# The state space stage of a hybrid encoder layer, reordered as a pipeline over pairs of heads, with the PSUM banks shared out anew

## The chip, the cores and the metric

One core of one Trainium2 chip runs the whole layer as one program. The metric is the device time of one execution in microseconds; lower is better. The kernel before takes 2852.92 us (median of three runs, 2851.68 to 2853.5). One execution was also taken by the hardware profiler; it took 2852.71 us, and 2850.9 us of that lie between its first and its last instruction (the span).

## The reference

One layer of a streaming encoder works on 384 tokens: 256 frames of a new stream and 8 running streams with 16 frames each. All is float32. The part that matters here is branch B, a state space model over 64 heads in 8 groups:

```python
proj = u @ p['w_in']                    # pool | z | x,B,C | dt | gates
xbc  = silu(causal_conv(xbc) + b)
dt   = softplus(dt_raw + dt_bias);  A = -exp(a_log)
def step(h, inp):                       # one chunk of 64 frames, all heads
    cum   = jnp.cumsum(dtc * A, axis=1)
    decay = jnp.exp(jnp.where(causal, cum[:, :, None] - cum[:, None, :], -jnp.inf))
    cb    = jnp.einsum('btgn,bsgn->btsg', Cc, Bc)
    xdt   = xc * dtc[..., None]
    y = einsum('btsgr,bsgrp->btgrp', cb[..., None] * decay, xdt)
    y = y + einsum('btgn,bgrpn->btgrp', Cc, h) * jnp.exp(cum)[..., None]
    h = h * exp(last) + einsum('bsgn,bsgr,bsgrp->bgrpn', Bc, exp(last - cum), xdt)
...
y = y + d_skip * xh
a_ssd = rmsnorm_per_group(y * silu(z)) * ssd_norm
m = sigmoid(g_A) * (A @ w_pool_proj) + sigmoid(g_B) * (a_ssd @ w_ssd_proj)
x += rmsnorm(m @ w_out);  x += rmsnorm(relu(rmsnorm(x) @ w_up)**2 @ w_down)
```

The outputs are the 384 tokens and the new pooling, convolution and state space states.

## The kernel before

**Matrix products.** Channels lie on the partitions and the 384 tokens along the free axis. A weight comes as units of 128x1024 float32 by the DMA queue of the sync engine (SP), through three buffers (`wfetch`, L62). ScalarE rounds it to the type fp32r (`wh`, L72), VectorE computes what is lost by that (`wl`, L74); both go through three buffers too. One 128x128 block then takes three matmuls, `wh*xh`, `wh*xl` and `wl*xh` (`mm3`, L80 to L83). A projection of 128 channels (`proj`, L94) reads two units and is 48 matmuls of 128x384 into one PSUM bank.

**Order.** A scheduler at build time orders each engine's instructions by its own estimate of when their inputs are ready; the engines then issue in that fixed order and wait on semaphores. `tc.issue_after` (`behind`, L59) keeps one instruction behind another on its engine. A pool gives out its buffers in the order in which the program asks.

**PSUM.** The eight banks are two pools of four: `psm` (`mmtile`) for all projections and for the products of the MLP, `pss` (`sstile`) for transposes, norms and the state space products.

**Stages in order.** First the tokens are loaded and the first projections run, with the input norm `rstd`. Then come the pooling branch (`pool_tile`, `pool_map`: tiles pj_p, pw, dh), gates (pj_ga), `dt_phase` (L291) and the pooling output (pj_pp). `dt_phase` computes softplus and the cumulated sums on VectorE (L299 to L329) and transposes the results with eleven small transposes to PSUM (`tk`, L341), from which `tok` is copied.

Then the state space stage, L409 to L601, loops over eight groups of heads:

- ten projections: B and C (`conv`: evacuation, convolution of four taps, SiLU), four x (also `conv`), four z;
- B's transposes (`trB`, L428), from which `Bk` and, by way of DRAM, the block-diagonal `bst` are made; C masked by stream (`Cm`); the products B C (`cb`, L452), masked to `cbm`;
- for each of two pairs of 128 channels (four heads): the old state `hs` and the cumulated sums `cbc` are loaded; x is transposed (`trx`, L475) and scaled to `xdt` and `xdw`; `yi` (L480) is C times the old state, eight products of 32 columns; the decays `E` (128x2048, L500 to L515) are made on ScalarE and VectorE; `Y` (L528) is twelve products of `xdt` with `E`; `yis`, the scaled yi, is added to Y by a product with the identity (L538); `pp` (L542) is the new state of the first stream; `su` (L581) that of the other eight, from `bst` and from `xst`, which also goes by way of DRAM (`xscr`);
- `finish` (L586): the norm over the group (`norm_bc`, with its product `bc`), the results to DRAM;
- one gate projection (`gate_b`) in the first six groups, the others behind the loop.

trB, trx, cb, yi, Y, L538 and pp are true float32 products; projections and su are fp32r. The program writes a group's products behind its ten projections; the scheduler then mixes them with the projections that follow.

Last come the output of branch B (pj_sp), w_out (wo), the second norm and the MLP. At the MLP's entry, x1 is transposed tile by tile (`trm`, L727), split to `x1h` and `x1l`, and its squares are summed on ScalarE (L743) for the norm, whose product `bc` is at L749; the first MLP projection (pj_up, L763) follows in the program.

Of the kernel before, what the change touches and what calls it, by code (L numbers as in the profile page):

```python
# [14 lines left out]
P = 128  # L15
T = 384
# [18 lines left out]
def build(ctx, tc, io):  # L35
# [5 lines left out]
    psm = ctx.enter_context(tc.tile_pool(name="psm", bufs=4, space=PSUM))  # L41
    pss = ctx.enter_context(tc.tile_pool(name="pss", bufs=4, space=PSUM))
# [41 lines left out]

    def half(o, q, wl_, rhs):
        h, l = wl_
        for k in range(8):
            i = q * 8 + k
            c = slice(k * P, k * P + P)
            last[0] = mm3(o, h[:, c], l[:, c], rhs[i][0], rhs[i][1], i == 0, i == len(rhs) - 1)  # L90

    last = [None]
# [69 lines left out]
    wt = mmtile("warm_o")  # L162
# [16 lines left out]
    ps = mmtile("pj_p0")[:, :T]  # L179
    ps1 = mmtile("pj_p1")[:, :T]  # L180
# [27 lines left out]
    with tc.tile_pool(name="phc", bufs=1, reuse_waits="tile") as pc, tc.tile_pool(name="phc2", bufs=2, reuse_waits="tile") as pc2:  # L208
# [153 lines left out]
    with tc.tile_pool(name="phd", bufs=2, reuse_waits="tile") as pd, tc.tile_pool(  # L362
# [46 lines left out]
        for g in range(G):  # L409
            u0 = 49 + g * 10  # L410
            BT = conv(u0, 32 + g, "BT", 2)
            CT = conv(u0 + 1, 40 + g, "CT", 2)
            xs = []
            for j in range(4):
                xs.append(conv(u0 + 2 + j, g * 4 + j, "xs", 6))
                if g and j == 2:
                    finish(last[0])
            zs = []
            for j in range(4):
# [4 lines left out]
                zs.append(z)  # L424

            tr = sstile(f"trB{g}")
            for b in range(3):
                te.transpose(tr[:, b * P : b * P + P], BT[:, b * P : b * P + P], ident)  # L428
            Bk = pd.tile([P, 2, P], F32, tag="Bk", name=f"Bk{g}")
            s.copy(Bk.rearrange("p b n -> p (b n)"), tr[:, :TP])  # L430
            Bhl = pd.tile([P, 2, P], F32R, tag="Bhl", name=f"Bhl{g}", bufs=1)
            s.activation(Bhl[:, 0, :], tr[:, TP:T], AF.Copy)
            v.tensor_tensor(Bhl[:, 1, :], tr[:, TP:T], Bhl[:, 0, :].bitcast(F32), ALU.subtract)
            bscr = b_scr[g]
            sy.dma_start(bscr, Bhl.bitcast(F32))
            bs = bst[g % 2]
            for p4 in range(4):
                for h2 in range(2):
                    sy.dma_start(
                        bs[p4 * 32 + h2 * 16 : p4 * 32 + h2 * 16 + 16, :, h2, :].bitcast(F32),  # L440
                        bscr.rearrange("(q h r) l n -> h l r q n", q=4, h=2)[h2, p4 // 2],
                    )
            Cm = pd.tile([P, 2, P], F32, tag="Cm", name=f"Cm{g}")
            v.tensor_tensor(
                Cm,
                CT[:, TP:].unsqueeze(1).to_broadcast([P, 2, P]),
                cst[:, C_CM : C_CM + 256].rearrange("p (a t) -> p a t", a=2),
                ALU.mult,
            )
            cb = sstile(f"cb{g}")  # L450
            for sb, t0, c0, n in ((0, 0, 0, 256), (1, P, 256, P), (2, TP, T, P)):
                te.matmul(  # L452
                    cb[:, c0 : c0 + n], BT[:, sb * P : sb * P + P], CT[:, t0 : t0 + n], start=True, stop=True
                )
            cbm = pd.tile([P, 512], F32, tag="cbm", name=f"cbm{g}")
            v.tensor_tensor(cbm, cb, cst[:, C_MASK : C_MASK + 512], ALU.mult)

            ssum = pd.tile([P, T], F32, tag="ssum", name=f"ssum{g}", bufs=1)
            for jp in range(2):
                nm = f"{g}_{jp}"  # L460
                qd = g * 2 + jp
                h0 = qd * 4
                js = (jp * 2, jp * 2 + 1)
                hs = pd.tile([P, NB, 2 * P], F32, tag="hs", name=f"hs{nm}")
                sy.dma_start(hs, io["ssm"][qd])
                cbcs = []
                for q in range(2):
                    cbc = pd.tile([P, 2, T], F32, tag="cbc", name=f"cbc{nm}_{q}")
                    sy.dma_start(cbc, cum_scr[h0 + q * 2 : h0 + q * 2 + 2, :].partition_broadcast(P))
                    cbcs.append(cbc)  # L470
                trs = []
                for j in js:
                    tr = sstile(f"trx{g}_{j}")
                    for b in range(3):
                        te.transpose(tr[:, b * P : b * P + P], xs[j][:, b * P : b * P + P], ident)  # L475
                    trs.append(tr[:, :T].rearrange("p (b h q) -> p b h q", b=3, h=2))
                yi = sstile(f"yi{nm}")
                for c in range(4):
                    for r in range(2):
                        te.matmul(  # L480
                            yi[c * 32 : c * 32 + 32, :256],
                            Cm[:, r, c * 32 : c * 32 + 32],
                            hs[:, 2 * c + r, :],
                            start=r == 0,
                            stop=r == 1,
                        )
                xdt = pd.tile([P, 2, 3, P], F32, tag="xdt", name=f"xdt{nm}", bufs=1)
                xdw = pd.tile([P, 2, 3, P], F32, tag="xdw", name=f"xdw{nm}", bufs=1)
                for q, tv in enumerate(trs):
                    for o, i in ((xdt, 3), (xdw, 6)):  # L490
                        v.tensor_tensor(
                            o[:, q].rearrange("p b (h q) -> p b h q", h=2),
                            tv,
                            tok[:, i : i + 3, h0 + q * 2 : h0 + q * 2 + 2].unsqueeze(3).to_broadcast([P, 3, 2, 64]),
                            ALU.mult,
                        )
                xhl = pd.tile([P, 2, 2, P], F32R, tag="xhl", name=f"xhl{nm}", bufs=1)
                s.activation(xhl[:, 0], xdw[:, :, 2, :], AF.Copy)
                v.tensor_tensor(xhl[:, 1], xdw[:, :, 2, :], xhl[:, 0].bitcast(F32), ALU.subtract)
                E = pd.tile([P, 4, 512], F32, tag="E", name=f"E{nm}", bufs=1)  # L500
                for hh in range(4):
                    ch = cbcs[hh // 2][:, hh % 2]
                    s.activation(E[:, hh, P:TP], ch[:, P:TP], AF.Exp, bias=tok[:, 9, h0 + hh : h0 + hh + 1])
                    for b, e0 in enumerate((0, TP, T)):
                        v.tensor_scalar(
                            E[:, hh, e0 : e0 + P],
                            ch[:, b * P : b * P + P],
                            tok[:, b, h0 + hh : h0 + hh + 1],
                            0.0,
                            ALU.subtract,  # L510
                            ALU.min,
                        )
                s.activation(E[:, :, :P], E[:, :, :P], AF.Exp)
                s.activation(E[:, :, TP:], E[:, :, TP:], AF.Exp)
                v.tensor_tensor(E, E, cbm.unsqueeze(1).to_broadcast([P, 4, 512]), ALU.mult)  # L515
                yis = pd.tile([P, 2, P], F32, tag="yis", name=f"yis{nm}", bufs=1)
                v.tensor_tensor(
                    yis.rearrange("p j (h q) -> p (j h) q", h=2),
                    yi[:, :256].rearrange("p (h q) -> p h q", h=4),
                    tok[:, 10, h0 : h0 + 4].unsqueeze(2).to_broadcast([P, 4, 64]),  # L520
                    ALU.mult,
                )
                Ys = []
                for q in range(2):
                    Y = sstile(f"Y{nm}_{q}")
                    for sb, e0, c0, n in ((0, 0, 0, TP), (1, TP, P, P), (2, T, TP, P)):
                        for hh in range(2):
                            te.matmul(  # L528
                                Y[hh * 64 : hh * 64 + 64, c0 : c0 + n],
# [65 lines left out]
            if g == G - 1:  # L595
                finish(None)
            if g < NG:
                gate_b()
# [331 lines left out]
```

## Time and profile before

| what | value |
|---|---|
| median of three runs | 2852.92 us |
| profiled execution | 2852.71 us |
| its span | 2850.9 us |
| matmul records | 15855 |
| granted TensorE clock, mean | 0.998 |
| VectorE, ScalarE, GpSimd busy | 55%, 38%, 4% |
| chain that ended last: share of TensorE | 96% |
| one group of heads, from 648.34 to 754.70 | 106.36 us |
| from there, VectorE and ScalarE busy | 81.82 us, 48.93 us |

In the profile, PE is the TensorE matmul and PEld its weight load, DVE is VectorE, ACT ScalarE, POOL GpSimd and SP the sync engine. A timeline line has the start in us, the length, the engine, the line of the kernel, the operation, what it writes and reads, shapes and count; in square brackets stand the idle time ahead of it and what ended that. Matmuls are pipelined, so that a record is longer than the distance to the next start; the starts tell the pace. A float32 product has two records, a transpose or an fp32r product one. A line of the table by stretches has the stretch, its length, the busy time of PE, PEld, DVE, ACT and POOL with their counts, the granted TensorE clock (1.00 is full), the share of the DMA engines and GB/s.

### The profile page before, as it was taken

What the parts mean: (1) busy time and instruction counts of PE and PEld (TensorE: products, weight loads), DVE (VectorE), ACT (ScalarE), POOL (GpSimd) and SP (SyncE); (2) the same over time, 40 slices, a digit from 0 to 9 for tenths busy, and PEclk for the clock granted to TensorE, in tenths of its full rate; (3) what the DMA queues carried; (4) which work ended last, traced back from release to release, by engine and by line L of the source; (5) the groups of instructions that cost most, each with busy time, mean ns of one, the idle gap of its engine ahead of it and who ended that gap; (6) DMA issues with size and microseconds to landing.
All of it is one profiled execution on the core that took longest, in us unless ns stands there. A gap on an engine that the chain in (4) does not pass through costs nothing.

```text
span 2850.9 us, 39369 instructions
## 1 busy us (share of the span) xinstructions
PE 2828.8 (99%) x15855; PEld 2676.3 (94%) x15855; DVE 1569.1 (55%) x2235; ACT 1081.7 (38%) x1554; POOL 105.0 (4%) x156
## 2 busy tenths in 40 slices
PE   8999999999999999999999999999999999999998
PEld 7999999999999999999999987989898998989897
DVE  7674335678778778777533334534444444444445
ACT  5343224345345345344422233533232333323233
POOL 0000000001001001011000000000000000000000
PEclk9999999999999999999999999999999999999999
DMA  6444445466466466466644453343343343344333
GB/s 204 138 133 142 137 138 195 143 213 213 155 211 217 156 206 219 159 212 231 205 152 155 143 182 115 133 131 126 128 129 128 126 130 129 126 128 130 127 126 126
DMA packets 141655, 448.78 MB, mean 157 GB/s; under 512 B 17200, under 2 KB 40816, under 8 KB 136864
## 3 DMA queue, kind: packets, MB, share of 16 engines
q1 hardware_dynamic: 133152, 410.14, 44.4%
q0 software_dynamic: 8320, 36.13, 3.3%
q8 instruction: 124, 2.03, 0.3%
q14 instruction: 59, 0.48, 0.1%
HBM read 404.48 MB, written 41.72 MB: 157 GB/s over the span
## 4 chain that ended last, share of the span: by engine, by line
PE 96%; DVE 2%; issue 1%; ACT 1%; DMA 0%; SPq 0%; DVEq 0%; ACTq 0%
PE pj_up L82 6%; PE pj_up L83 6%; PE pj_up L81 6%; PE wd L645 6%; PE wd L644 6%; PE wd L646 6%; PE pj_x L81 5%; PE pj_x L83 5%; PE pj_x L82 5%; PE pj_sp L81 3%; PE pj_z L82 3%; PE pj_sp L83 3%; PE pj_z L81 3%; PE pj_sp L82 3%; PE pj_z L83 3%; PE pj_gb L81 2%
## 5 line engine op out<-in xcount | busy, mean ns | idle before, releaser
L81 PE MATMUL pj_up<-x1h,wh_up 128*128 128x384 f32 x1024 | 343.3, 335 | 0.0
L82 PE MATMUL pj_up<-x1l,wh_up 128*128 128x384 f32 x1024 | 342.9, 335 | 0.0
L83 PE MATMUL pj_up<-x1h,wl_up 128*128 128x384 f32 x1024 | 342.8, 335 | 0.0
L74 DVE TENSOR_TENSOR wl_wd<-w_wd,wh_wd 128x1024 fp32r<-128x1024 f32 x127 | 155.7, 1226 | 261.9 <-ACT wh_wd L72 261.9
L645 PE MATMUL wd<-wl_wd,hh 128*128 128x512 f32 x762 | 296.6, 389 | 0.0
L646 PE MATMUL wd<-wh_wd,hl 128*128 128x512 f32 x762 | 296.6, 389 | 0.0
L644 PE MATMUL wd<-wh_wd,hh 128*128 128x512 f32 x762 | 296.3, 389 | 0.0
L72 ACT ACTIVATE wh_wd<-w_wd 128x1024 fp32r<-128x1024 f32 x127 | 134.8, 1061 | 350.7 <-PE wd L646 284.2
L74 DVE TENSOR_TENSOR wl_up<-w_up,wh_up 128x1024 fp32r<-128x1024 f32 x128 | 156.7, 1225 | 198.7 <-ACT wh_up L72 198.7
L72 ACT ACTIVATE wh_up<-w_up 128x1024 fp32r<-128x1024 f32 x128 | 135.7, 1062 | 325.5 <-PE pj_up L82 264.8
L81 PE MATMUL pj_x<-xgh,wh_x 128*128 128x384 f32 x768 | 258.2, 336 | 0.0
L82 PE MATMUL pj_x<-xgl,wh_x 128*128 128x384 f32 x768 | 257.8, 336 | 0.0
L83 PE MATMUL pj_x<-xgh,wl_x 128*128 128x384 f32 x768 | 257.6, 335 | 0.0
L81 PEld LDWEIGHTS pj_up<-x1h,wh_up 128*128 128x128 f32 x1024 | 192.6, 188 | 0.8 <-ACT x1h L731 0.4
L82 PEld LDWEIGHTS pj_up<-x1l,wh_up 128*128 128x128 f32 x1024 | 192.6, 188 | 0.4
L83 PEld LDWEIGHTS pj_up<-x1h,wl_up 128*128 128x128 f32 x1024 | 192.6, 188 | 0.0
L83 PE MATMUL pj_z<-xgh,wl_z 128*128 128x384 f32 x512 | 171.0, 334 | 0.0
L81 PE MATMUL pj_z<-xgh,wh_z 128*128 128x384 f32 x512 | 171.0, 334 | 0.0
L82 PE MATMUL pj_z<-xgl,wh_z 128*128 128x384 f32 x512 | 171.0, 334 | 0.0
L81 PE MATMUL pj_sp<-abh,wh_sp 128*128 128x384 f32 x512 | 171.0, 334 | 0.0
L82 PE MATMUL pj_sp<-abl,wh_sp 128*128 128x384 f32 x512 | 171.0, 334 | 0.0
L83 PE MATMUL pj_sp<-abh,wl_sp 128*128 128x384 f32 x512 | 171.0, 334 | 0.0
(289 smaller groups left out, 6056.5 us busy)
## 6 DMA issues: line engine op xcount, KB each, us to landing
w_up<-w_up SPq DMA_DIRECT2D x128, 512.0 KB, 3.4
w_wd<-w_down SPq DMA_DIRECT2D x128, 512.0 KB, 3.4
w_x<-w_in SPq DMA_DIRECT2D x96, 512.0 KB, 4.5
w_z<-w_in SPq DMA_DIRECT2D x64, 512.0 KB, 4.3
w_sp<-w_ssd SPq DMA_DIRECT2D x64, 512.0 KB, 3.5
w_ga<-w_in SPq DMA_DIRECT2D x32, 512.0 KB, 3.4
w_pp<-w_pp SPq DMA_DIRECT2D x32, 512.0 KB, 3.4
hs<-ssm SPq DMA_DIRECT2D x16, 1024.0 KB, 6.0
```

Of the source, the lines that this page charges most:

```text
L72: s.activation(h, w, AF.Copy)
L74: v.tensor_tensor(l, w, h.bitcast(F32), ALU.subtract)
L81: te.matmul(out, wh, xh, start=first, stop=False)
L82: te.matmul(out, wh, xl, start=False, stop=False)
L83: return te.matmul(out, wl, xh, start=False, stop=last)
L644: te.matmul(o[b], mh, wh[:, c], start=k == 0, stop=False)
L645: te.matmul(o[b], mh, wl[:, c], start=False, stop=False)
L646: te.matmul(o[b], ml, wh[:, c], start=False, stop=k == nk - 1)
```

## The change

PSUM is split into two banks (`psm`) and six (`pss`). Within the state space stage projections use `psm`; everywhere else they now use `pss`, as all the other tiles do. Within the stage all matmuls are chained by `issue_after` in the program's order, and the program's order is a pipeline: a group's products stand in two runs. The first comes behind the third x projection: trB, then transposes of yis, Y and pp of the previous group's second pair, then cb, trx and yi of this group's first pair. The second comes behind the fourth z: yis, Y and pp of the first pair, trx and yi of the second. The yis are now transposed straight into Y's bank, ahead of Y's products, which add to them. pp and yi share a bank. The products su stand behind the third z and behind C's projection of the next group. E is made in two halves, and the loads of hs and cbc and the way by DRAM of xst are placed anew. The computations are those of before.

```diff
-    psm = ctx.enter_context(tc.tile_pool(name="psm", bufs=4, space=PSUM))
-    pss = ctx.enter_context(tc.tile_pool(name="pss", bufs=4, space=PSUM))
+    psm = ctx.enter_context(tc.tile_pool(name="psm", bufs=2, space=PSUM))
+    pss = ctx.enter_context(tc.tile_pool(name="pss", bufs=6, space=PSUM))
...
+    last = [None]
+    bank = [sstile]
+    chain = [False]
+
     def half(o, q, wl_, rhs):
         h, l = wl_
-        for k in range(8):
...
+        with behind(last[0] if chain[0] else None):
+            for k in range(8):
...
     def proj(units, rhs, name):
-        o = mmtile(f"pj_{name}")[:, :T]
+        o = bank[0](f"pj_{name}")[:, :T]
...
-    wt = mmtile("warm_o")
+    wt = sstile("warm_o")
...
-                    o = mmtile(f"pw{n}")[:, :T]
+                    o = sstile(f"pw{n}")[:, :T]
...
+        def lump(fn):
+            with behind(last[0]):
+                last[0] = fn()
...
+        def t_yT(S):
+            for q in range(2):
+                Y = sstile(f"Y{S.nm}_{q}")
+                i = te.transpose(Y[:, TP:T], S.yis[:, q], ident)
...
+        def t_Y(S):
...
-                                start=sb == 0,
-                                stop=False,
+                            start=False,
+                            stop=sb > 0,
...
-                    te.matmul(Ys[q][:, TP:T], yis[:, q], ident, start=False, stop=True, skip_group_check=True)
...
+        bank[0] = mmtile
+        chain[0] = True
+        prev = None
+        for g in range(G + 1):
...
+            D.BT = conv(u0, 32 + g, "BT", 2)
+            pload(D.p[0])
+            if g:
+                dside(prev.p[1])
+            D.CT = conv(u0 + 1, 40 + g, "CT", 2)
+            if g:
+                state(prev.p[1])
+            D.xs.append(conv(u0 + 2, g * 4, "xs", 6))
+            cload(D.p[0])
+            cside(D)
+            D.xs.append(conv(u0 + 3, g * 4 + 1, "xs", 6))
+            D.xs.append(conv(u0 + 4, g * 4 + 2, "xs", 6))
+            S = D.p[0]
+            lump(lambda: t_trB(D))
+            bside(D)
+            if g:
+                lump(lambda: t_yT(prev.p[1]))
+                lump(lambda: t_Y(prev.p[1]))
+            S.py = sstile(f"py{S.nm}")
+            if g:
+                lump(lambda: t_pp(prev.p[1], S.py))
+            lump(lambda: t_cb(D))
+            lump(lambda: t_trx(S))
+            lump(lambda: t_yi(S))
+            if g:
+                final(prev.p[1])
+            xside(S)
+            mside(D)
+            D.xs.append(conv(u0 + 5, g * 4 + 3, "xs", 6))
+            eside(S, 0)
...
+            zproj(0)
+            if g:
+                finish(prev)
+            pload(D.p[1])
+            eside(S, 1)
+            zproj(1)
+            dside(S)
+            zproj(2)
+            state(S)
+            cload(D.p[1])
+            zproj(3)
+            S1 = D.p[1]
+            lump(lambda: t_yT(S))
+            lump(lambda: t_Y(S))
+            S1.py = sstile(f"py{S1.nm}")
+            lump(lambda: t_pp(S, S1.py))
+            lump(lambda: t_trx(S1))
+            lump(lambda: t_yi(S1))
+            final(S)
+            xside(S1)
+            if g < NG:
+                gate_b()
+            eside(S1, 0)
+            eside(S1, 1)
+            prev = D
+        bank[0] = sstile
+        while gates:
+            gate_b()
+        chain[0] = False
...
-            o = [mmtile(f"wo{nb}_{b}") for b in range(3)]
+            o = [sstile(f"wo{nb}_{b}") for b in range(3)]
...
-                    ps = mmtile("pj_up0")[:, :T]
+                    ps = sstile("pj_up0")[:, :T]
...
-                o = [mmtile(f"wd{c8}_{nb}_{b}") for b in range(3)]
+                o = [sstile(f"wd{c8}_{nb}_{b}") for b in range(3)]
```

The new helpers hold the lines of before: `pload` and `cload` the loads of hs and cbc; `bside`, `cside`, `mside` those that make Bk and bst, Cm, and cbm; `xside` xdt, xdw, yis, xhl and the way to xst; `eside` one half of E; `dside` the decay of hs; `state` su with its sums; `final` the copy of pp, the skip, the product with z and the sum of squares. When the eight groups are done, the rest of the last pair stands among four gates, and six gates follow.

More of the change, by code (lines that the diff above doesn't have):

```diff
@@ new lines, in build, with pload, cload, t_trB @@
+        class Pair:
+            pass
+        def pload(S):
+            S.hs = pd.tile([P, NB, 2 * P], F32, tag="hs", name=f"hs{S.nm}")
+            sy.dma_start(S.hs, io["ssm"][S.qd])
+        def cload(S):
+            S.cbcs = []
+            for q in range(2):
+                cbc = pd.tile([P, 2, T], F32, tag="cbc", name=f"cbc{S.nm}_{q}")
+                sy.dma_start(cbc, cum_scr[S.h0 + q * 2 : S.h0 + q * 2 + 2, :].partition_broadcast(P))
+                S.cbcs.append(cbc)
+        def t_trB(D):
+            D.tr = sstile(f"trB{D.g}")
+            for b in range(3):
+                i = te.transpose(D.tr[:, b * P : b * P + P], D.BT[:, b * P : b * P + P], ident)
+            return i
@@ new lines, in t_cb, with t_trx @@
+        def t_cb(D):
+            D.cb = sstile(f"cb{D.g}")
+            for sb, t0, c0, n in ((0, 0, 0, 256), (1, P, 256, P), (2, TP, T, P)):
+                i = te.matmul(
+                    D.cb[:, c0 : c0 + n], D.BT[:, sb * P : sb * P + P], D.CT[:, t0 : t0 + n], start=True, stop=True
+                )
+            return i
+        def t_trx(S):
+            S.trs = []
+            for j in S.js:
+                tr = sstile(f"trx{S.g}_{j}")
+                for b in range(3):
+                    i = te.transpose(tr[:, b * P : b * P + P], S.D.xs[j][:, b * P : b * P + P], ident)
+                S.trs.append(tr[:, :T].rearrange("p (b h q) -> p b h q", b=3, h=2))
+            return i
@@ new lines, in t_yi @@
+        def t_yi(S):
+            S.yi = S.py[:, 256:]
+            for c in range(4):
+                for r in range(2):
+                    i = te.matmul(
+                        S.yi[c * 32 : c * 32 + 32, :],
+                        S.D.Cm[:, r, c * 32 : c * 32 + 32],
+                        S.hs[:, 2 * c + r, :],
+                        start=r == 0,
+                        stop=r == 1,
+                    )
+            return i
+        def t_yT(S):
+            S.Ys = []
+            for q in range(2):
+                Y = sstile(f"Y{S.nm}_{q}")
+                i = te.transpose(Y[:, TP:T], S.yis[:, q], ident)
+                S.Ys.append(Y)
+            return i
@@ new lines, in t_pp, with bside @@
+        def t_pp(S, py):
+            S.pp = py[:, :256]
+            for q in range(2):
+                for b in range(2):
+                    i = te.matmul(
+                        S.pp[:, q * P : q * P + P], S.xdw[:, q, b, :], S.D.Bk[:, b, :], start=b == 0, stop=b == 1
+                    )
+            return i
+        def bside(D):
+            D.Bk = pd.tile([P, 2, P], F32, tag="Bk", name=f"Bk{D.g}")
+            s.copy(D.Bk.rearrange("p b n -> p (b n)"), D.tr[:, :TP])
+            Bhl = pd.tile([P, 2, P], F32R, tag="Bhl", name=f"Bhl{D.g}", bufs=1)
+            s.activation(Bhl[:, 0, :], D.tr[:, TP:T], AF.Copy)
+            v.tensor_tensor(Bhl[:, 1, :], D.tr[:, TP:T], Bhl[:, 0, :].bitcast(F32), ALU.subtract)
+            bscr = b_scr[D.g]
+            sy.dma_start(bscr, Bhl.bitcast(F32))
+            D.bs = bst[D.g % 2]
+            for p4 in range(4):
+                for h2 in range(2):
+                    sy.dma_start(
+                        D.bs[p4 * 32 + h2 * 16 : p4 * 32 + h2 * 16 + 16, :, h2, :].bitcast(F32),
+                        bscr.rearrange("(q h r) l n -> h l r q n", q=4, h=2)[h2, p4 // 2],
+                    )
@@ new lines, in dside, with state, t_su @@
+        def dside(S):
+            v.tensor_tensor(
+                S.hs.rearrange("p b (h q) -> p b h q", h=4),
+                S.hs.rearrange("p b (h q) -> p b h q", h=4),
+                decb[:, S.h0 : S.h0 + 4, :].rearrange("p h b -> p b h").unsqueeze(3).to_broadcast([P, NB, 4, 64]),
+                ALU.mult,
+            )
+        def state(S):
+            def t_su():
+                for r in range(4):
+                    su = sstile(f"su{S.nm}_{r}")
+                    for b in range(2):
+                        i = te.matmul(
+                            su[:, b * 256 : b * 256 + 256], S.D.bs[:, r, b, :], S.xst[:, r, :], start=True, stop=True
+                        )
+                    hr = S.hs[:, r * 2 : r * 2 + 2, :].rearrange("p b n -> p (b n)")
+                    v.tensor_tensor(hr, hr, su, ALU.add)
+                return i
+            lump(t_su)
+            gp.dma_start(io["new_ssm_s"][S.qd], S.hs)
@@ new lines, in finish, with pair @@
+        def finish(D):
+            bc = norm_bc(pd, D.ssum, 512, f"g{D.g}", last[0])
+            for j in range(4):
+                i = D.g * 4 + j
+                z = D.zs[j]
+                v.scalar_tensor_tensor(
+                    out=z, in0=z, scalar=vec[:, V_NRM + i : V_NRM + i + 1], in1=bc, op0=ALU.mult, op1=ALU.mult
+                )
+                gp.dma_start(a_scr[i], z)
+        def pair(D, jp):
+            S = Pair()
+            S.D, S.g, S.jp, S.js = D, D.g, jp, (jp * 2, jp * 2 + 1)
+            S.nm, S.qd = f"{D.g}_{jp}", D.g * 2 + jp
+            S.h0 = S.qd * 4
+            return S
@@ L423, in build @@
                 s.activation(z, z, AF.Silu)
[L424 to L454, printed above, removed]
@@ L586, in finish @@
[L586 to L596 removed]
+                D.zs.append(z)
```

266 lines of the change are left out of this document (117 added, 149 removed).

## The prediction

> **What bounds the kernel now.** I read the page first, for the busy shares; then the table by stretches, for the price of one group; then the timeline of TensorE, for what stands between two matmuls.
>
> ```profile
> PE 2828.8 (99%) x15855; PEld 2676.3 (94%) x15855; DVE 1569.1 (55%) x2235; ACT 1081.7 (38%) x1554; POOL 105.0 (4%) x156
> ```
>
> ```profile
> 648.34:754.70 106.36, 106.26 (x673) 102.55 (x672) 81.82 (x132) 48.93 (x80) 9.32 (x12) 1.00 0.59 194
> ```
>
> TensorE (PE) is never free, and inside one group of heads (106.36 us, the second line, columns PE, PEld, DVE, ACT, POOL) it is busy for 106.26 us. VectorE has 24.5 us to spare in the group. So a microsecond goes away only where TensorE issues less or waits less, and every microsecond it is made to wait anywhere in the kernel is added to the end.
>
> A busy PE is not yet a PE at its peak, so I go by the distance between starts. Projections: 630.06 to 647.74 in the timeline holds 102 matmuls, 0.1733 us each. A group has 528 (ten projections and one gate, 48 each): 91.5 us. That leaves 14.9 us per group for the state space products.
>
> ```profile
> 655.88 0.34 PE L82 MATMUL pj_gb<-xgl,wh_gb 128*128 128x384 f32 x1
> 656.14 1.96 PE L528 MATMUL Y<-E,xdt 128*64 128x256 f32 x24
> 658.03 0.71 PE L538 MATMUL Y<-cst,yis 128*128 128x128 f32 x4
> 658.58 1.06 PE L542 MATMUL pp<-Bk,xdw 128*128 128x128 f32 x8
> 659.39 0.42 PE L83 MATMUL pj_gb<-xgh,wl_gb 128*128 128x384 f32 x1
> 659.65 0.33 PE L81 MATMUL pj_gb<-xgh,wh_gb 128*128 128x384 f32 x1
> ```
>
> The first column is the start. Y takes 1.89, the two fp32 products with the identity (L538, two records each) 0.55, pp 0.81. A projection next to an fp32 product costs 0.26 (655.88 to 656.14, 659.39 to 659.65) where 0.173 would do: 0.09 for each change of form. In the same way trB is 0.33, cb 0.88, a pair's six trx 0.57, yi 1.02, a pair's su 0.96.
>
> **The state space stage.** The changed program's TensorE order puts each group's products in two unbroken runs. The first: trB 0.33, two transposes of yis 0.22 (trx gives 0.11 for one; they replace L538), Y 1.89, pp 0.81, cb 0.88, trx 0.57, yi 1.02: 5.7. The second lacks trB and cb: 4.5. su twice 1.9, the norm's bc 0.35, and six changes of form at 0.09 make 0.5: 13.1 against 14.9. Of the 1.8 saved, 0.7 is L538 becoming transposes and 1.1 is changes of form that vanish (before, trx, yi and Y of the second pair stand singly among projections). Eight groups: **-14.4 us**.
>
> What could take it back is a wait. The products' inputs are made 3 to 5 projections (8.3 us each) ahead. With two banks for projections, the evacuation must come within 8.3 us of a projection's end; with three weight buffers, each half's low part (L74, 1.2 us) must be ready every 4.16 us. I added up VectorE's new order with the durations of before (E 0.27 each, its product with the mask 1.1 per half, conv 0.55 + 0.42 + 3 x 0.62, hs 2.28, norm about 5.6 + 2.4). The longest queue stands behind the first run: rest of a conv, final, xside, mask, E, about 10 us before the next weight half. The tightest halves (second half of z_1, first of z_3) come 3 to 4 us before TensorE asks; the slowest evacuation has about 4 us left. Seven tiles go through six banks in the first run; the seventh (the second trx) reuses trB's bank, which VectorE leaves about 3 us into the run, 1.5 us before it is wanted. SP's queue now holds xscr's write ahead of the weights of z_2; it waits about 4 us for its partner, as the one of before does, and the weights are wanted 10 us later. So I cost all this at nothing; should one of these covers fail, it is about 1 to 2 us per group.
>
> **The dt phase.** The rest of the diff is not in that stage: every other PSUM tile now comes from one pool. The new order shows what that does. Before, the transposes of dt (tk) are issued in the midst of pj_pp, 113 matmuls behind pj_dt. Now tk stands directly behind pj_dt and pj_pp waits behind it, on an engine that issues in order. Before:
>
> ```profile
> 199.00 0.55 DVE L299 TENSOR_TENSOR raw<-pj_dt,rstd 64x384 f32<-64x384 f32 x1 [2.02 <-PE pj_dt L83]
> ...
> 202.65 2.54 DVE L303 RECIPROCAL t<-t 64x384 f32<-64x384 f32 x1
> ...
> 206.20 0.54 DVE L304 TENSOR_TENSOR t<-e,t 64x384 f32<-64x384 f32 x1
> ...
> 218.06 0.94 DVE L315 TENSOR_TENSOR_SCAN cum<-cst,dta 64x384 f32<-64x384 f32 x1
> ...
> 220.57 0.55 DVE L329 TENSOR_TENSOR dtw<-dt,we 64x384 f32<-64x384 f32 x1 [0.59 <-ACT we L328]
> ```
>
> This chain is what tk needs. Up to the reciprocal's end (205.2) nothing changes. From 206.20 to the scan's end at 219.0 it takes 12.8, of which 4.35 are five other instructions (three L74, ma, gat) that now stand behind it; about 0.4 of that overlapped. So the scan ends at 205.2 + 12.8 - 4.35 + 0.4 = 214.05, dtw 2.1 later (219.04 to 221.12 before), the last five transposes take 0.45: pj_pp starts at 216.6, not 198.80. TensorE loses 17.8. Against that, tk and its wait (0.84 at 218.22) cost 1.9 before: 198.80 to 222.66 is 23.86 us with 127 projection matmuls in it, 22.0. Net +15.9.
>
> **The clock behind a gap.** Before has one long wait of TensorE in mid-kernel, 3.21 us ahead of 1777.52:
>
> ```profile
> 1777.00:1780.00 3.00, 2.13 (x6) 1.22 (x6) 3.00 (x6) 1.96 (x5) 0.00 (x0) 0.54 0.00 0
> 1780.00:1783.00 3.00, 2.96 (x13) 2.79 (x13) 2.30 (x5) 2.31 (x7) 0.56 (x1) 0.50 0.50 191
> 1783.00:1785.00 2.00, 2.00 (x13) 1.87 (x13) 1.19 (x3) 1.78 (x5) 0.00 (x0) 0.73 0.58 238
> ```
>
> The third column from the right is the granted clock: half speed from 1777.2 to 1784.1, 6.8 us. At half speed TensorE loses half the time: up to 3.4. It was only partly busy there. At the kernel's start the first 128x512 matmuls stand 0.43 apart (0.227 later), from 2.55 until about 5.7 with dense work: a loss of 1.6. I take 2.4 for a gap. [...] dt phase: **+18.3 us**.
>
> **The entry of the MLP.** Here too one pool changes the order: all sixteen trm, then the norm's bc, then pj_up. Before, pj_up fills in between trm and stands ahead of bc:
>
> ```profile
> 1777.52 1.12 PE L727 MATMUL trm<-cst,x 128*128 128x128 f32 x4 [3.21 <-DVE x L717]
> 1778.67 1.01 PE L81 MATMUL pj_up<-x1h,wh_up 128*128 128x384 f32 x2
> ...
> 1796.77 0.88 PE L749 MATMUL bc<-dg,cst 128*128 128x384 f32 x2
> 1797.20 0.63 PE L81 MATMUL pj_up<-x1h,wh_up 128*128 128x384 f32 x1
> ```
>
> By 1796.70 before has issued 63 matmuls of pj_up; the changed kernel none: 63 x 0.1733 = 10.9. bc waits for ScalarE: sixteen x1h (0.47 apart) and twelve squares (0.61 apart), from 1778.04 to 1794.3, then 2.3 us of small steps. That work stays, and gaps in it (0.5 + 0.4 at 1782 and 1783, where half-speed pj_up stood between trm) mostly go: bc about 1 us earlier, some of which its half speed takes back, -0.8. A TensorE that idles from about 1786 to 1795.6 comes back at half speed: +2.4. Sum **+12.5 us**.
>
> **The start.** With six banks, the fifth projection no longer waits for the first one's bank (0.80 idle before 45.73, 0.96 by starts): **-1.0 us**; the wait for dh that follows (before 55.7) may eat it.
>
> **Sum.** -14.4 + 18.3 + 12.5 - 1.0 = +15.4 on the span of 2850.9. The profiled execution took 2852.71, so 1.8 lie around the span, and the median of 2852.92 is 0.2 above it. Forecast: **2868 us**, 0.5% slower.
>
> **Rivals.**
> - *The stage itself stalls too.* A half of the weights, or a bank, comes late by 1 to 2 us in every group: +12, 2880. For it: VectorE is at 77% in the stage and its work is lumped. Against it: 3 us of room as added up. Chance 0.12.
> - *One of the two gaps is covered.* If pj_pp, or pj_up, starts as early as before, the sum is -2.9 or +2.9: 2850 to 2856. Against it: the order leaves nothing to issue in between. Chance 0.08.
> - *Faster: TensorE passes a waiting matmul.* If matmuls whose inputs are there overtake tk and bc, both gaps close and only the stage's gain stays: 2852.7 - 15.4 = 2837. It decides once overtaking hides 25 of the 30.8 us. Against it: at 218.22 the next pj_pp matmul is ready, yet issues at 219.57, behind tk. Chance 0.05.
> - *The change does not do what it says*: the runs break up, or changes of form cost the same when packed, and the stage gains only 5.3 (L538): 2877. It lies within my range; chance 0.08.
>
> The forecast keeps 0.67: 2861 to 2876, from the bounds of the clock (1.6 to 3.4 per gap), of the dt chain (1 us either way), of pj_up's start (1.5) and of the stage (-16 to -11). The range of 2858 to 2880 takes in the slower cases and leaves out the two that close a gap. This kernel's measurement tells about 0.2%, 5.7 us, from no change: slower 0.87, same 0.08, faster 0.05.
>
> **What would show it.** A group of 104.5 us with two runs of products; no wait of TensorE in it; a hole of about 17 us behind pj_dt and one of about 9 between trm and bc; half clock behind both. It is wrong if the group stays at 106, or if either hole is missing.

## The result and the profile after

The changed kernel takes 2871.48 us (median of six runs, 2869.22 to 2872.7) against 2852.97 us of the kernel before (six runs): a ratio of 1.0065 with a 95% interval of 1.0052 to 1.0078. It is slower, by 18.5 us; 2868 was forecast. The profiled execution took 2871.82 us, its span 2870.1 us, at a mean granted clock of 0.993 (0.998 before).

The line of the page that answers to the first one above:

```profile
PE 2824.9 (98%) x15823; PEld 2680.8 (93%) x15823; DVE 1568.9 (55%) x2251; ACT 1095.1 (38%) x1590; POOL 96.5 (3%) x156
```

TensorE is busy for 4 us less in a span that is 19 us longer: the time went into waits. The view of TensorE's waits of the kernel after names them (in us: total, number, longest):

```profile
PE tk L345 <- DVE cum L319: 15.1, 1, 15.1
PE bc L881 <- DVE dg L879: 10.3, 1, 10.3
PE warm_o L168 <- POOL warm L164: 2.6, 1, 2.6
PE trm L859 <- DVE x L849: 2.4, 2, 2.0
```

Two single waits make up 25 us. Taken for the state space stage alone, where 16 blocks of products were moved, the view lists no wait. The timeline of TensorE after, at both places:

```profile
195.96 0.34 PE L83 MATMUL pj_dt<-xgh,wl_dt 128*128 128x384 f32 x1
211.40 0.58 PE L345 MATMUL tk<-cst,cum 64*128 64x64 f32 x3 [15.10 <-DVE cum L319]
211.77 0.53 PE L345 MATMUL tk<-cst,dt 64*128 64x64 f32 x3
213.51 0.58 PE L345 MATMUL tk<-cst,dtw 64*128 64x64 f32 x3 [1.22 <-DVE dtw L333]
213.89 0.42 PE L345 MATMUL tk<-cst,nb 64*128 64x64 f32 x2
214.24 0.69 PE L81 MATMUL pj_pp<-ah,wh_pp 128*128 128x384 f32 x1
...
1789.70 2.66 PE L859 MATMUL trm<-cst,x 128*128 128x128 f32 x18
1802.63 1.62 PE L881 MATMUL bc<-dg,cst 128*128 128x384 f32 x2 [10.27 <-DVE dg L879]
1803.48 1.09 PE L81 MATMUL pj_up<-x1h,wh_up 128*128 128x384 f32 x1
```

pj_pp needs nothing of tk, and pj_up needs nothing of bc; both stand behind it. One steady group takes 105.16 us, against 106.36 before. Its line in the table by stretches of the kernel after:

```profile
618.21:723.37 105.16, 105.16 (x669) 102.36 (x668) 81.80 (x134) 51.09 (x85) 8.32 (x12) 1.00 0.59 196
```

The two runs of products stand in that group as planned. TensorE's timeline of its second run, with the first projection behind it:

```profile
667.41 0.38 PE L471 MATMUL Y<-cst,yis 128*128 128x128 f32 x2
667.72 1.96 PE L479 MATMUL Y<-E,xdt 128*64 128x256 f32 x24
669.60 1.16 PE L493 MATMUL py<-Bk,xdw 128*128 128x128 f32 x8
670.60 0.82 PE L450 MATMUL trx<-cst,xs 128*128 128x128 f32 x6
671.35 1.09 PE L458 MATMUL py<-hs,Cm 128*32 128x256 f32 x16
672.37 0.44 PE L81 MATMUL pj_gb<-xgh,wh_gb 128*128 128x384 f32 x1
```

The first line there are the transposes of yis (yT below), and py holds first pp, then yi.

The difference between the two profiles, cut where the same product starts in both (pj_dt's last, first pj_x, first pj_sp, first trm, end):

| part | forecast | measured |
|---|---|---|
| start, to pj_dt's last product | -1.0 | -2.67 |
| dt phase, to the first pj_x | +18.3 | +18.94 |
| state space stage, to the first pj_sp | -14.4 | -9.22 |
| pj_sp, wo | 0 | 0 |
| MLP, from the first trm | +12.5 | +12.06 |
| sum | +15.4 | +19.12 |

### The profile page after: what moved, and what is told of

Read it like the earlier page. It is cut to its first block, busy times and chain, and to the rows that moved or that the text cites. A ratio compares the mean times of both kernels' runs of the same rounds, so it can differ in the third digit from the quotient of the medians.

```text
span 2870.1 us, 39341 instructions
## 1 busy us (share of the span) xinstructions
PE 2824.9 (98%) x15823; PEld 2680.8 (93%) x15823; DVE 1568.9 (55%) x2251; ACT 1095.1 (38%) x1590; POOL 96.5 (3%) x156
```

## The experiments

All times are medians; the kernel before took 2852.83 to 2853.16 us beside them. The names e1 to e11 stand for the kernels.

### e1, e2, e3: the holes closed

e1: the two-bank pool serves the projections from the first gate tile on and is kept to the end. e2 has only the first of these, with the first line of the diff; e3 only the second, with the rest.

```diff
+        bank[0] = mmtile
         sg = gate_a(0)
...
-        bank[0] = sstile
         while gates:
...
-                    ps = sstile("pj_up0")[:, :T]
+                    ps = mmtile("pj_up0")[:, :T]
```

> The changed kernel, with the two-bank pool used for the products from the first gate tile ahead of the dt phase on and kept to the end, so that the dt transposes and the MLP's entry (transposes and broadcast) have the six-bank pool to themselves. Theory (the loss is two holes in TensorE's order, made where products share a pool with work that waits for VectorE): both holes go, about -19 in the dt phase and -12 at the MLP's entry against the changed kernel's 2871.5, and the stage's gain of 9.2 and the start's of 2.7 stay, so about 2841, faster than both kernels. Rival 1 (two banks are too few for products outside the stage): the products of the pool map's gate, the pp tiles and the up tiles wait for their evictions; a wait of some 0.5 us at each of the 16 + 16 products of the first part and the 64 of the MLP would give 2850 or more. Rival 2 (the chain ahead of the dt transposes is itself the limit): pj_pp starts early, but the hole appears later, and the time stays above 2860.

> The changed kernel with the dt phase alone put back: products take the two-bank pool from the first gate tile to the end of the stage, and the six-bank pool after it. Theory: first pj_pp product at about 196 instead of 214 us, no half clock behind it, about -19: 2852 to 2853, and the hole of 10.5 us at the MLP's entry stays as it is. Rival (the chain is the limit, or two banks are too few): less than -10, so over 2861.

> The changed kernel with the MLP's entry alone put back: the two-bank pool is kept for the products behind the stage, and the first up tile takes it too. Theory: the up products run between the transposes and ahead of the broadcast's product, the hole of 10.5 us at 1792 goes, about -12: 2859 to 2860; the dt hole of 15.4 us stays. Rival (the broadcast's wait moves to the up tiles' evictions, which need its result): the products stop at the second up tile, and the gain is under 5: over 2866.

Measured: e1 2841.92 us (2840.87 to 2843.48), ratio to before 0.9961, interval 0.9947 to 0.9975; e2 2852.85, ratio 0.9999 (0.9989 to 1.0008); e3 2861.36, ratio 1.0029 (1.0018 to 1.0041). Against the kernel after that is -29.6, -18.6 and -10.1. From pj_dt's last product to the first pj_x, e1 and e2 take as long as before (260.08 and 260.10 us, before 260.07). The timeline of TensorE in e1 shows why:

```profile
215.48 0.34 PE L82 MATMUL pj_pp<-al,wh_pp 128*128 128x384 f32 x1
216.32 0.40 PE L345 MATMUL tk<-cst,cum 64*128 64x64 f32 x3 [0.50 <-DVE cum L319]
216.56 0.35 PE L345 MATMUL tk<-cst,dt 64*128 64x64 f32 x3
216.84 0.44 PE L83 MATMUL pj_pp<-ah,wl_pp 128*128 128x384 f32 x1
```

With its own pool, tk goes back into the midst of pj_pp, 20.4 us behind pj_dt, and waits 0.5. Both holes were made by which tiles share a pool, and not by the stage or by too few banks: e1 runs its projections from 196 us on with two banks and beats both kernels, and e8 below, with four banks and four and the pools as in e1, has neither hole. e3 fell 1.4 to 2.4 us short. The MLP of e1 still costs 1.15 more than before. Ahead of bc stand 56 up products instead of 63, and TensorE waits there, in the timeline of e1:

```profile
1784.69 0.88 PE L881 MATMUL bc<-dg,cst 128*128 128x384 f32 x2 [1.30 <-DVE dg L879]
```

In e8 there are 63 and no such wait, so the split of the banks does this. It is worth little: the MLP of e8 still costs 0.70 more than before, and its bc comes 0.6 later. The MLP of e3 costs 2.49 more than before. It has the same 56 products and the same wait, its bc comes 0.7 later than in e1, and 0.6 fall among the down products (one wait of 0.4 there). The 6.8 us at half clock at its entry begin 5.5 us behind the first trm, in e1 3.9; whether that makes bc late is not shown.

### e4, e11: the old stage with the new pools

The kernel before with two and six banks, its projections inside the stage on two. Every other tile takes the six. In e4, whose diff this is, the gates behind the last group take the six-bank pool again; in e11 the last line stands behind their loop, and they take the two banks.

```diff
-    psm = ctx.enter_context(tc.tile_pool(name="psm", bufs=4, space=PSUM))
-    pss = ctx.enter_context(tc.tile_pool(name="pss", bufs=4, space=PSUM))
+    psm = ctx.enter_context(tc.tile_pool(name="psm", bufs=2, space=PSUM))
+    pss = ctx.enter_context(tc.tile_pool(name="pss", bufs=6, space=PSUM))
+    bank = [sstile]
...
-        o = mmtile(f"pj_{name}")[:, :T]
+        o = bank[0](f"pj_{name}")[:, :T]
...
+        bank[0] = mmtile
         for g in range(G):
...
+        bank[0] = sstile
         while gates:
             gate_b()
```

> The stage's old program with the new pools: two banks for its projections and six for everything else, in the kernel and in its stage. Theory (the pools make the loss, the new stage program the gain): the dt hole and the MLP's hole are there as in the changed kernel, +19 and +12 on 2853.0, the start gives -2.7, and the old stage is as it was: about 2881. Rival 1 (the old stage gains or loses by the split itself, since its fp32 work gets six banks and its projections two): the stage differs by more than 2 us from the 1273.3 us between its first pj_x product and the first one behind it in the kernel before. Rival 2 (the holes come from the new program's explicit order of products, not from the pools): about 2850 to 2853.

(The 1273.3 in it is a slip: that stretch is 917.05 us in the kernel before.) Measured: 2900.0 us, 19 more than expected. The dt phase (+18.3) and the MLP (+12.7) came as foreseen; the stage took 936.76 us, and all of the excess lies in its last group: 214.47 us to the first pj_sp against 193.96, while a steady group took 106.02. TensorE's timeline in e4, there:

```profile
1292.85 1.09 PE L482 MATMUL yi<-hs,Cm 128*32 128x256 f32 x16
1298.19 3.68 PE L530 MATMUL Y<-E,xdt 128*64 128x256 f32 x24 [4.25 <-DVE E L517]
...
1307.41 2.04 PE L583 MATMUL su<-xst,bst 128*128 128x256 f32 x8 [3.13 <-DMA xst<-x_scr]
...
1324.56 2.04 PE L583 MATMUL su<-xst,bst 128*128 128x256 f32 x8 [5.44 <-DMA xst<-x_scr]
1326.40 0.52 PE L108 MATMUL bc_g<-nh_g,onesr 128*128 128x384 f32 x1
...
1327.22 0.49 PE L81 MATMUL pj_gb<-xgh,wh_gb 128*128 128x384 f32 x1
```

The gates' products, which filled these waits before, stand behind the whole group. This is a third hole, which e4 itself made; e11 puts that to the test.

> The old stage program with the new pools (2900.0), but the products of the last ten gates, which stand behind the last group, take the two-bank pool too. In the run before they stood in TensorE's order behind the last group's whole work, since they shared the six banks with it, and that stretch was 20.5 us longer than in the kernel before. Theory (a third hole of the same kind, by the pool alone): the last group comes back to 194 us and the time to about 2880. Rival (the old stage is slow at its end because of the two banks of the projections): over 2895.

Measured: 2877.09 us, last group 192.09 us. The theory holds: in all three places of this study, products that share a pool with work that waits are put behind it. e11 also says what the split alone does for the old stage: 914.38 us, 2.7 less than before; the new program brings 6.6 more.

### e5: the transposes of yis undone

```diff
-                i = te.transpose(Y[:, TP:T], S.yis[:, q], ident)
+                i = te.matmul(Y[:, TP:T], S.yis[:, q], ident, start=True, stop=True)
```

> The changed kernel with the scaled yi brought into Y's bank by an fp32 product with the identity, first in the bank, in place of the transpose. In the kernel before these products took 0.137 us an instruction pair row (0.548 for the four records of a pair of tiles) against 0.31 for the two transposes. Theory (the transposes are cheaper by 0.2 to 0.33 us a pair of heads, less what the change of form behind them costs): 16 pairs times 0.2 to 0.33, +3 to +5 against the changed kernel's 2871.5, so 2874.5 to 2877. Rival (the change of form behind the transposes eats their gain): within 2 of 2871.5.

Measured: 2876.06 us (2873.51 to 2877.93), +4.6; the stage 911.69 us, +3.87, and a steady group 105.63 against 105.15. The pair took 0.54 us where the two transposes take 0.31. The transposes bring 0.48 us a group, not the 0.66 of the forecast: two transposes side by side cost 0.22 (e6 below), and ahead of Y 0.31.

### e6, e10: products of one form side by side

Both start from e1. The diff is the second block's. In e6 the blocks are trB, yT, trx, pp, cb, yi, Y and yT, trx, pp, yi, Y (yT: the transposes of yis). In e10 the first is trB, pp, cb, trx, yT, yi, Y, and the last group keeps its old second block.

```diff
             lump(lambda: t_yT(S))
-            lump(lambda: t_Y(S))
+            lump(lambda: t_trx(S1))
             lump(lambda: t_pp(S, S1.py))
-            lump(lambda: t_trx(S1))
             lump(lambda: t_yi(S1))
+            lump(lambda: t_Y(S))
```

> The kernel with both holes closed (2841.9), and inside the two blocks of the stage products of one form put side by side: first block trB, yT, trx, pp, cb, yi, Y; second block yT, trx, pp, yi, Y. Theory (each change of form costs about 0.1 us on either side of it, and this is the 0.45 us a block by which the stage fell short): two changes fewer in a block, -0.2 to -0.35 a block, 16 blocks: -3 to -5.5, so 2836.5 to 2839. Rival 1 (a change of tile width, from 32 columns to 64, costs as much as a change from transposes to products): within 1.5 of 2841.9. Rival 2 (with Y last in the block, final and the scaling of x and yi come later, and a product waits): over 2843.

Measured: 2852.87 us, 11 slower than e1: rival 2. In the second block the change of order did what was meant, 4.77 us against 4.96; in the first a wait came. The waits of TensorE in e6, then its timeline there:

```profile
PE cb L441 <- DVE Bhl L504: 5.0, 7, 0.7
PE su L591 <- DMA xst<-x_scr: 4.2, 1, 4.2
```

```profile
598.95 0.49 PE L435 MATMUL trB<-cst,xs 128*128 128x128 f32 x3
...
600.15 1.06 PE L494 MATMUL py<-Bk,xdw 128*128 128x128 f32 x8
601.92 1.14 PE L441 MATMUL cb<-xs,xs 128*128 128x256 f32 x6 [0.72 <-DVE Bhl L504]
```

cb asks for the seventh bank, that of trB, and VectorE leaves it 2.97 us into the block. In the last group su waits for the transfer of x; with Y last, the work ahead of xside ends later. In e10, which keeps the old order there, that wait is gone.

> The kernel with both holes closed (2841.9), forms put side by side, mended: in the first block trB, pp, cb, trx, yT, yi, Y, so that the seventh bank asked for is that of trB 2.5 us after it; in the second block yT, trx, pp, yi, Y; the last group's second block as it was, since behind it the product for the state waited 4.2 us for the transfer of x. Theory: the second block saves the 0.194 us that the first try showed (4.768 against 4.962), the first block one change of form, 0.1 to 0.19, and nothing waits: 7 groups by 0.3 to 0.38, -2 to -2.7, so 2839 to 2840, and a steady group at 104.75 to 104.85 instead of 105.15 us. Rival (with Y last, the bank or the vector work of the next product still comes late): a steady group over 105.15 and the time over 2842.

Measured: 2840.93 us (2838.69 to 2841.44), ratio 0.9955 (0.9943 to 0.9968), the fastest kernel of this study, by no more than its spread. A steady group takes 104.94, -0.21, less than the 0.3 to 0.38 expected: the second block gives 0.19 again, the first almost nothing: pp and trx give 0.1 each, and yT, now between trx and yi, takes 0.17 of it back (0.48 against 0.31); why it is dearer there stays open. TensorE's timeline in e10, second block:

```profile
649.06 0.38 PE L472 MATMUL Y<-cst,yis 128*128 128x128 f32 x2
649.28 0.82 PE L451 MATMUL trx<-cst,xs 128*128 128x128 f32 x6
649.94 1.06 PE L494 MATMUL py<-Bk,xdw 128*128 128x128 f32 x8
650.92 1.09 PE L459 MATMUL py<-hs,Cm 128*32 128x256 f32 x16
651.94 1.96 PE L480 MATMUL Y<-E,xdt 128*64 128x256 f32 x24
653.83 0.44 PE L81 MATMUL pj_gb<-xgh,wh_gb 128*128 128x384 f32 x1
```

By starts, trx takes 0.66 here, with a change of form on one side, and 0.75 in the kernel after, with one on each side (0.57 without any, by the prediction): 0.09 to 0.1 us for each, inside a block as next to a projection.

### e7, e9: the hole filled, to measure the clock

The changed kernel with products that nothing uses ahead of the transposes of dt: the order stays, only TensorE is kept at work. e9 has 17 of them, and 12 of 128x128 in the second, short wait.

```diff
+                for _ in range(16 if r == 0 else 0):
+                    te.matmul(o, ident, cst[:, C_MASK : C_MASK + 512], start=True, stop=True)
                 for i, a in enumerate(part):
                     te.transpose(o[:, i * NH : i * NH + NH], a, ident[:NH, :NH])
```

> The changed kernel with the dt hole filled by work that is not used: 16 fp32 products of 128x512 into the transposes' bank ahead of them, some 0.9 us each by the rate of cb, 14 us of the 15.4 us hole. The order stays, only TensorE is kept busy, so what it brings is the clock's share. Theory (of the +19.0 of the dt phase some 2.8 are half clock behind the hole): the first pj_pp product stays at 214, the 87 products behind it lose 2.8 less: about 2868.7. Rival (the clock is granted by something else than TensorE's idle time, or the price stands in other places): within 1 of 2871.5.

> The changed kernel with the dt hole filled again by work that is not used, and the second short wait inside it too: 17 fp32 products of 128x512 ahead of the first transposes (0.86 us each as the first filling measured) and 12 of 128x128 ahead of the transposes of dtw. With the first filling the granted clock stayed whole through the hole, and only one stretch of 3413 ns at half remained, behind the two waits of 1.9 and 1.75 us. Theory (the clock is set stretch by stretch of 3413 ns by how much TensorE worked; no stretch is idle enough any more): no half clock between 190 and 300 us, the dt phase at +16 instead of +18.9 on the kernel before, and about 2868.5. Rival (one stretch at half follows whatever fills the hole, because the waits between the products remain): half clock for 3413 ns or more behind 210 us, dt phase at +17 or more, and the time within 1.5 of 2871.5.

Measured: 2871.54 and 2870.31 us against 2871.48. Both are the numbers of the rivals; the times alone can't tell what the clock did. The traces can. The table by stretches (third column from the right: granted clock) of the kernel after, of e7 and of e9:

```profile
200.50:211.00 10.50, 0.00 (x0) 0.00 (x0) 9.98 (x16) 0.00 (x0) 0.00 (x0) 0.50 0.09 35
...
214.00:217.40 3.40, 3.40 (x13) 3.28 (x13) 0.96 (x2) 0.00 (x0) 0.00 (x0) 0.50 0.22 77
217.40:220.80 3.40, 3.40 (x14) 3.40 (x13) 0.00 (x0) 0.00 (x0) 0.00 (x0) 0.59 0.02 5
```

```profile
200.50:211.00 10.50, 9.12 (x24) 3.85 (x23) 9.95 (x18) 0.26 (x2) 0.00 (x0) 1.00 0.01 3
...
214.00:217.40 3.40, 3.40 (x13) 3.40 (x12) 0.21 (x1) 0.00 (x0) 0.00 (x0) 0.53 0.24 77
```

```profile
200.50:211.00 10.50, 10.50 (x26) 4.61 (x25) 9.42 (x15) 0.56 (x2) 0.00 (x0) 1.00 0.15 50
...
214.00:217.40 3.40, 3.40 (x31) 3.21 (x30) 1.28 (x3) 0.39 (x1) 0.00 (x0) 1.00 0.14 30
```

At half clock the products of pj_pp start 0.32 us apart, where dense ones at full clock take 0.1733. The timeline of TensorE in the kernel after:

```profile
217.28 0.52 PE L81 MATMUL pj_pp<-ah,wh_pp 128*128 128x384 f32 x1
217.60 0.52 PE L82 MATMUL pj_pp<-al,wh_pp 128*128 128x384 f32 x1
```

In e9 no half clock is left between 190 and 300 us, and from pj_pp's first product to the first pj_x 258.03 us pass, 260.74 in the kernel after: the clock's share is 2.7 us, which is also what 5.9 us at that pace lose, and the other 16.2 of the dt phase are the gap. e9's own filling runs 1 us past the hole (pj_pp starts 19.3 us behind pj_dt instead of 18.3), which hides part of that in the time; the dt phase is +17.2, so the number of the rival came, for another reason than its own.

### e8: four banks and four

e1 with PSUM split as before.

```diff
-    psm = ctx.enter_context(tc.tile_pool(name="psm", bufs=2, space=PSUM))
-    pss = ctx.enter_context(tc.tile_pool(name="pss", bufs=6, space=PSUM))
+    psm = ctx.enter_context(tc.tile_pool(name="psm", bufs=4, space=PSUM))
+    pss = ctx.enter_context(tc.tile_pool(name="pss", bufs=4, space=PSUM))
```

> The kernel with both holes closed (2841.9), with PSUM split 4 and 4 as in the kernel before: the start and the whole stage program then have four banks for everything that is not a product of weights. Theory 1 (the six banks carry the stage's block, which takes seven banks in turn, and the start): the start loses its 2.7 again, and in each group's first block trx waits for Y's eviction, 1 to 2 us in each of the 7 groups that have a Y there: 2851 to 2858. Theory 2 (only the pools' membership matters, not their sizes): 2842 to 2845, the start's share alone.

Measured: 2852.35 us, +10.4 on e1, theory 1. The stage takes 918.78 us, +10.94, and a steady group 106.58. TensorE's waits in e8:

```profile
PE trx L451 <- DVE xs L611: 8.3, 7, 1.2
```

Once per group the second trx waits 1.2 us for Y's bank, which the sum with x (L611) leaves. Neither hole comes back (260.05 us from pj_dt's last product to the first pj_x): which tiles share a pool makes them, and not the number of its banks. Without the six banks the new program would be no faster than the old one: 918.78 against 917.05. The start, in turn, gave nothing that the medians show: the stage alone is more than the whole difference.

## Why the prediction was right, and where its sizes were off

**Direction and mechanism: right, and shown.** e1 to e4, e8 and e11 show that the loss is the two gaps and that the pools make them. That the total came within 3.5 us is in part luck: the stage gained 5.2 less than forecast, and the start took 1.7 of that back.

**The dt phase: right.** The forecast put the scan's end 15.4 us behind pj_dt's last product and pj_pp 18.0 behind it; measured were 15.44 (to tk) and 18.28. The gap cost +16.2 (15.9) and the clock 2.7 (2.4): the dense products ran at half clock for 5.9 us, from 214.24 to 220.17.

**The MLP's entry: right,** +12.06 against +12.5. No pj_up stood ahead of bc; bc came 1.2 us earlier against the first trm (0.8 to 1 forecast), and bc and the products behind it ran 4.7 us at half clock, a loss of 2.2 (from bc to the twelfth pj_up product behind it 4.86 us, 2.63 before).

**The stage: the mis-sized term.** -14.4 was forecast, -9.2 measured, outside the -16 to -11 that the forecast allowed. This error of 5.2 us is larger than the whole miss of 3.5. (The terms of the sum as written make 13.0 a group, not 13.1; by them the stage would have gained 15.2, still further off.) The step that failed is "six changes of form at 0.09 make 0.5": it counted those at the ends of the runs and took the products inside at the price they have among their own kind. In the kernel after, the first run takes 6.17 us (5.7) and the second 4.96 (4.5): yT 0.31 (0.22), pp 0.995 (0.81), trx 0.75 (0.57). The 0.45 a run that is too much stands in these three, at the joints with products of another form, and is five times the 0.09 of one change. At the ends the cost was smaller than the 0.5 allowed, so that a group gains 1.2 and not 1.8. e10, which takes two of the changes out of the second run, gives back 0.19; e5 sizes the transposes at 0.48 a group instead of 0.66. Packing does away with changes between projections and the rest, and the ones among the packed products stay.

**What was costed at nothing: right, and the room was as narrow as said.** No wait came in the stage. The forecast let VectorE leave trB's bank about 3 us into the run; e6, which asks for it earlier, measured 2.97. e8 took that cover away and paid 1.2 us per group, the "1 to 2 us" named.

**The start: right in sign, not settled in size.** -2.67 by one pair of profiles. The wait for the first bank went (0.8 us before, absent after). But e8, with four banks, has no wait at that place either, and the first pw product came between 53.49 and 56.03 us in eleven profiles of kernels with six banks (55.71 in the one of before, 57.40 in e8), so that part is within the scatter. From the first pw product to pj_dt's last, 142.92 us passed before and 141.4 to 141.5 in all others, e8 with its four banks too: those 1.45 us are not the number of banks. They lie in the first 48 pw products, which start unevenly before, once waiting for dh (0.23 at 59.72): these took 9.97 us before, 8.59 in e8, and in the kernel after 9.00 with three pj_p products among them. Behind them the same number of products takes the same time. Why they start unevenly before stays open.

**The rivals.** The stage did not stall; neither gap was covered; TensorE passed no waiting matmul (pj_pp stood behind tk, the inputs of its first half made by 190.8, until 214.24). "The stage gains only 5.3" names what was off: the stage's gain came out about half way between it and the forecast.

## What to carry to other kernels

A pool of PSUM tiles is also an order: where a builder's scheduler works through a pool in the order of requests, a product that shares it with tiles that wait for another engine is put behind that wait: here 15.1 us ahead of tk, 10.3 ahead of bc, and in e4 a last group that is 20.5 us longer. When banks are shared out anew for one stage, look at every other stage that uses the pool, and give products of weights and tiles that wait on vector work separate pools everywhere. Here two banks were nearly enough for the products (the MLP of e1 took 1.15 us more than before, that of e8 with four banks 0.70), and the same change with that is 0.4% faster than before instead of 0.65% slower. When products are packed into blocks, count a change of form at every joint inside the block (for trx here 0.09 to 0.1 us each), not only at its ends.

## What the runs showed of the hardware that was not expected

**Half clock came in whole multiples of 3413 ns.** In the records of the granted clock read here, each stretch at half speed in mid-kernel lasted a multiple of that: in the kernel before 6827 ns at the MLP's entry (two); in the dt phase 20480 ns in the kernel after (six), 17067 in e3 and e5 (five), 3413 in e7 (one); at the MLP's entry 6827 and 10240 in the kernel after, 3413 in e10. In the kernel after, the stretches that begin at 199.69 and 1783.47 us also lie 464 such steps apart; why they do was not shown. The same instructions did not lose the same time in every kernel: the dense products behind the dt hole ran 5.9 us at half clock in the kernel after and 2.7 in e3 (to 217.14, from 214.43), which at the two paces above (0.32 and 0.1733 us a product) makes 1.5 us of time. In e7, two waits of 1.38 and 1.53 us (ahead of 210.77 and 212.88) with little work between them were followed by 3413 ns at half, from 214.23 on. In the kernel after TensorE had only the transposes trm from 1787.09 to 1792.36, and the full clock came back at 1790.30, in the midst of them.

**fp32 products with the identity against transposes.** Two tiles of 128x128 took 0.54 us as products (e5), 0.22 as transposes among transposes (e6) and 0.31 as transposes ahead of Y (the kernel after).
